# Padding of the weight buffers, start addresses of y and the mix, and the last three pieces by block

## The chip, the cores and the metric

The kernel runs on one core of one Trainium2 chip. The metric is the device time of one execution in microseconds. The kernel before took 2162.01 us, the median of three runs (2161.94 to 2162.14).

## The reference

A two-layer encoder over 256 positions of width 2048, in float32. Every layer is a pre-norm attention and a SwiGLU block of width 5632, both residual; layer 0 has two groups of heads (chunked and differential attention), layer 1 has attention over keys that an indexer selects. Nearly all the arithmetic is in the weight matrices:

```python
for layer in range(DEPTH):
    h = rmsnorm(x, attn_norm[layer])
    ...                                   # projections of h, attention, output projection
    x = x + mix
    h = rmsnorm(x, ffn_norm[layer])
    x = x + (jax.nn.silu(h @ w_gate[layer]) * (h @ w_up[layer])) @ w_down[layer]
return rmsnorm(x, final_norm)
```

## The kernel before

Every weight matrix is streamed once, in pieces of 128 rows by 1024 float32 (two tiles of 128 rows by 512 columns). `load_w` brings a piece into `wl` by a DMA on SyncE's queue; ScalarE rounds it to `wh` (line 145) and VectorE makes the remainder `wo` = `wl` - `wh` (line 146), so that a product of two float32 matrices becomes three products of rounded parts. `wh` and `wo` have three buffers each, which the pieces take in turn. TensorE does nothing but matmuls, and every matmul has a load of its stationary operand ahead of it (PEld in the profile).

Two routines hold nearly all of the matmuls.

- `gemm_t` (tiles `acc`): the weights are the stationary operand, the activations `xs` the moving one. A piece serves four output tiles; for each there is a quartet: two matmuls of 512 columns with the two halves of `wh`, then two of 256 columns with the two halves of `wo` (function `products`). So a piece is 16 matmuls. The gate and up projections, the queries and the keys run here.
- `gemm_n` (tiles `nat`): the activations are the stationary operand and the weights, `wh` or `wo`, the moving one, always 512 columns. For each half of a piece and each block of 128 positions there is a triple (`mm3`): high part by `wh`, high part by `wo`, low part by `wh`. A piece is 12 matmuls. The values (stationary `xs` or `c`), the two output projections (stationary `mix`) and the down projections (stationary `y`) run here.

The order of the work is written out by hand: attention, norms and transposes are cut into steps that `pump` issues between matmuls. The end of the kernel is `finish_block`, once for each block of 128 positions: it adds the last column group to the residual (line 312), squares it and sums it (lines 307 and 271), makes the norm's factor (lines 255 and 257), scales four column groups (lines 674 to 678) and stores each (line 679). In the last down projection `gemm_n` is called with `last=2`: all but the last two pieces go block by block within a piece, and the last two go first for block 0, then `done` is called for it, and then for block 1.

Start addresses, in bytes within a partition, follow from the order and the sizes of the tiles. Counted by 256 they are, before:

| tile | start by 256 | used as |
|---|---|---|
| `xs` | 128 | moving in `gemm_t`, stationary for the values of layer 0 |
| `wh`, `wo` (4,224 bytes each, so every next buffer lies 128 further) | in two pieces of three `wh` 64 and `wo` 192, in the third `wh` 192 and `wo` 64 | stationary in `gemm_t`, moving in `gemm_n` |
| the same for pieces of the values (64 bytes on, `OFF`) | `wh` 128 and `wo` 0, or `wh` 0 and `wo` 128 | moving |
| `y` in both layers | 64 | stationary |
| `mix` of layer 0, of layer 1 | 64, 192 | stationary |

All steps inside these tiles (512, 1024 and 2048 bytes) are multiples of 256. A spacer tile ahead of `mix` (`SP0`, `SP1`) and of `y` (`SPY`) sets where these start.

Of the kernel before, what the change touches and what calls it, by code (L numbers as in the profile page):

```python
# [14 lines left out]
F32R = mybir.dt.float32r  # L15
# [5 lines left out]
P = 128  # L21
# [4 lines left out]
FT = DFF // P  # L26
# [13 lines left out]
def encoder_kernel(  # L40
# [27 lines left out]
    wpool = ctx.enter_context(tc.tile_pool(name="wpool", bufs=1))  # L68
# [13 lines left out]
    def bank(shape, name):  # L82
        return psum.tile(shape, F32, name=name, tag="ps")


    OFF = 16
    SP0, SP1, SPY = 16, 16, 96
    UKO, UVO = 0, OFF
    OUT0 = [4, 5, 6, 7, 0, 1, 2, 3]
    QUADS = (2, 3, 0, 1)  # L90
# [11 lines left out]
    def moving(pieces):  # L102
        return ((src, OFF) for src in pieces)

# [25 lines left out]
    def load_w(cuts=1, between=None):  # L130
        src = next(stream, None)
        if src is None:
            return
        src, off = src if isinstance(src, tuple) else (src, 0)
        if before:
            before.popleft()()
        width = src.shape[-1]
        wl = wpool.tile([P, width], F32, name="wl", tag="wl", bufs=5)
        wh, wo = (wpool.tile([P, width + 2 * OFF], F32R, name=n, tag=n, bufs=3)[:, off:off + width] for n in ("wh", "wo"))
        for i in range(cuts):  # L140
            if between is not None:
                between(i)
            c = slice(i * width // cuts, (i + 1) * width // cuts)
            nc.sync.dma_start(out=wl[:, c], in_=src[:, c])
            latest["act"] = nc.scalar.activation(wh[:, c], wl[:, c], AF.Copy)  # L145
            nc.vector.tensor_tensor(out=wo[:, c], in0=wl[:, c], in1=wh[:, c].bitcast(F32), op=ALU.subtract)  # L146
        ahead.append((wh, wo))

    def next_w():
        while len(ahead) < 3:  # L150
            n = len(ahead)
            load_w()
            if len(ahead) == n:
                break
        return ahead.popleft()
# [4 lines left out]
    def pump(n=1):  # L160
        for _ in range(n):
            while steps:
                try:
                    next(steps[0])
                    break
                except StopIteration:
                    steps.popleft()
# [15 lines left out]
    def mm3(out, a, b, start, stop):  # L183
        (ah, al), (bh, bl) = a, b
        mm(out, ah, bh, start, False)
        mm(out, ah, bl, False, False)
        mm(out, al, bh, False, stop)
# [26 lines left out]
    def gemm_n(lhs, nk, order=None, last=0, done=None):  # L214

        banks = [bank([P, 512], f"nat{i}") for i in range(2)]
        order = list(range(nk // 2)) if order is None else order

        def block_products(b, i, w):
            wh, wo = w  # L220
            for j in range(2):
                h, l = lhs(2 * order[i] + j)
                t = slice(b * P, (b + 1) * P)
                c = slice(j * 512, (j + 1) * 512)
                mm3(banks[b], (h[:, t], l[:, t]), (wh[:, c], wo[:, c]),
                    i == 0 and j == 0, i == len(order) - 1 and j == 1)

        for i in range(len(order) - last):
            w = next_w()
            for b in range(2):  # L230
                block_products(b, i, w)
                pump()
        if last:
            ws = [next_w() for _ in range(last)]
            for b in range(2):
                for i, w in enumerate(ws):
                    block_products(b, len(order) - last + i, w)
                done(b, banks[b])
        return banks

    def pairs(act):
        return lambda kt: (act[:, kt, 0, :], act[:, kt, 1, :])
# [59 lines left out]
    def new_sums():  # L302
        return {"sums": small.tile([P, 2, 4], F32, name="sums", tag="sums", bufs=2)}
# [5 lines left out]
    def add_block(bk, b, g, st):  # L309

        c = xn[:, b, 512 * g:512 * g + 512]
        nc.vector.tensor_tensor(out=c, in0=bk, in1=c, op=ALU.add)
        add_squares(st, b, g)
# [15 lines left out]
    def add_residual(banks, g, gi, st):  # L329
        for b in range(2):  # L330
            add_block(banks[b], b, g, st)
        steps.append(transpose_steps(g, gi))
# [30 lines left out]
    def load_x(t, n):  # L363
        if t:
            nc.sync.dma_start(out=xt[:, t:t + n, :], in_=xT[:, t:t + n, :])
        for i in range(t, t + n):
            normalize(i, xt[:, i, :], 0)

    load_w(2, between=lambda i: load_x(i, 1))
    before.extend(partial(load_x, t, 2) for t in range(2, KT, 2))  # L370
    load_w(2)
    load_w(2)

# [243 lines left out]
    def ffn(st):  # L617

        with tc.tile_pool(name="ffn", bufs=1) as fp:
            fp.tile([P, SPY], F32, name="spacer")  # L620
            y = fp.tile([P, FT, 2, S], F32R, name="y")
            for g in range(FT // 4):
                gb = gemm_t(xs, KT)
                if g == 0:
                    drain()
                ga = fp.tile([P, 4, S], F32, name="ga", tag="ga", bufs=1)
                for n in range(4):
                    a = ga[:, n, :]
                    combined(a, gb[n])
                    nc.vector.tensor_tensor(out=a, in0=a, in1=st["rr"], op=ALU.mult)  # L630
                    th = fp.tile([P, S], F32, name="th", tag="th", bufs=3)
                    nc.scalar.activation(th, a, AF.Tanh, scale=0.5)  # L632
                    nc.vector.scalar_tensor_tensor(out=a, in0=th, scalar=1.0, in1=a, op0=ALU.add, op1=ALU.mult)  # L633
                    nc.gpsimd.tensor_tensor(out=a, in0=a, in1=st["rs"], op=ALU.mult)  # L634
                ub = gemm_t(xs, KT)
                for n in range(4):
                    t = 4 * g + n
                    a = ga[:, n, :]
                    u = fp.tile([P, S], F32, name="up", tag="up", bufs=2)
                    combined(u, ub[n])  # L640
                    nc.vector.tensor_tensor(out=a, in0=a, in1=u, op=ALU.mult)
                    split((y[:, t, 0, :], y[:, t, 1, :]), a)
            yield y, fp

    def ffn_layer(st, gi, last):
        out = new_sums()
        body = ffn(st)
        y, fp = next(body)
        if last:
            gf = fp.tile([P, D], F32, name="gf", tag="ga", bufs=1)  # L650
            nc.sync.dma_start(out=gf, in_=bass.AP(tensor=gfin.tensor, offset=gfin.offset, ap=[[0, P], [1, D]]))
        for g in range(4):
            fin = last and g == 3
            banks = gemm_n(pairs(y), FT, last=2 if fin else 0, done=partial(finish_block, out, gf) if fin else None)
            if not last:
                add_residual(banks, g, gi, out)
            elif not fin:
                for b in range(2):
                    add_block(banks[b], b, g, out)
                    c = slice(512 * g, 512 * g + 512)  # L660
                    nc.gpsimd.tensor_tensor(out=xn[:, b, c], in0=xn[:, b, c], in1=gf[:, c], op=ALU.mult)
        for _ in body:
            pass
        return out
# [15 lines left out]

    steps.append(norm_steps(st, "n1", 0.5))
    st = ffn_layer(st, 2, False)


# [9 lines left out]
    banks = [bank([P, 2, S], f"x{n}") for n in range(3)]  # L694
# [135 lines left out]

    steps.append(norm_steps(st, "n3", 0.5))
    ffn_layer(st, 4, True)


# [61 lines left out]
```

## Time and profile before

| | |
|---|---|
| median of three runs | 2162.01 us |
| the profiled execution, its span | 2161.7 us, 2159.9 us |
| TensorE busy | 2148.4 us, 99% of the span |
| granted TensorE clock | 0.999 of full speed |
| VectorE, ScalarE, GpSimd busy | 60%, 49%, 8% |
| DMA, mean busy share by slices | 50 to 60% in nearly all slices |

The span runs from the first instruction to the last. A matmul's row in the trace starts when its columns enter and ends when they have left, so that rows of matmuls one after the other overlap: the step from one start to the next is shorter than a row. PE is TensorE's matmuls, PEld its loads of stationary operands, DVE VectorE, ACT ScalarE, POOL GpSimd, SP SyncE, which here only issues DMAs.

### The profile page before, as it was taken

To read this page: it belongs to the slowest core of one execution; us is meant where nothing else is said; L and a number is where in the kernel's file an instruction comes from. 1 tells how busy PE (TensorE), PEld (TensorE's weight loads), DVE (VectorE), ACT (ScalarE), POOL (GpSimd) and SP (SyncE) were. 2 spreads that over 40 slices of the span, in tenths; PEclk is the share of its full clock that TensorE was granted. 3 is DMA by queue.
4 is the path that set the end of the run, shared out by engine and by line. 5 is a ranking of instruction groups with operands and counts; after the bars stand their busy time and mean duration, and the time that the engine had idled before them with its cause. 6 is when DMAs were issued, how large, how long until landed. Compare 5 with 4: busy or idle time off the path is not lost.

```text
span 2159.9 us, 29908 instructions
## 1 busy us (share of the span) xinstructions
PE 2148.4 (99%) x11380; PEld 1836.1 (85%) x11380; DVE 1299.2 (60%) x1882; ACT 1065.6 (49%) x1603; POOL 178.6 (8%) x194
## 2 busy tenths in 40 slices
PE   9999999999999999999999999999999999999998
PEld 8888888888888888888888888888888888888886
DVE  6665555666666666544446977556666666654443
ACT  6554554545454454444435566445454454543443
POOL 0111000000000000000001241000000000000000
PEclk9999999999999999999999999999999999999999
DMA  9565556555555665555656554555555555566564
GB/s 319 174 178 167 175 167 184 184 186 186 189 188 189 187 188 191 186 185 187 193 168 214 166 156 151 182 186 186 189 189 188 187 189 190 186 207 193 187 193 138
DMA packets 114975, 401.95 MB, mean 186 GB/s; under 512 B 12618, under 2 KB 16526, under 8 KB 114702
## 3 DMA queue, kind: packets, MB, share of 16 engines
q1 hardware_dynamic: 114686, 399.90, 58.7%
q8 instruction: 89, 1.46, 0.3%
q14 instruction: 56, 0.46, 0.1%
q10 hardware_dynamic: 144, 0.13, 0.0%
HBM read 397.84 MB, written 2.14 MB: 185 GB/s over the span
## 4 chain that ended last, share of the span: by engine, by line
PE 98%; DMA 1%; DVE 0%; ACT 0%; issue 0%; SPq 0%; ACTq 0%; POOLq 0%; POOL 0%
PE acc L181 59%; PE nat L181 35%; PE x L181 1%; PE uk L181 1%; DMA xt<-in_xT 1%; PE xT L323 0%; PE is L181 0%; PE c3o L181 0%; PE a0o L181 0%; PE a1o L181 0%; PE c2o L181 0%; PE c0o L181 0%; PE c1o L181 0%; DVE wo L146 0%; PE b31o L181 0%
## 5 line engine op out<-in xcount | busy, mean ns | idle before, releaser
L146 DVE TENSOR_TENSOR wo<-wl,wh 128x1024 fp32r<-128x1024 f32 (+2 forms) x747 | 925.9, 1240 | 805.2 <-ACT wh L145 797.3
L145 ACT ACTIVATE wh<-wl 128x1024 fp32r<-128x1024 f32 (+2 forms) x747 | 786.9, 1054 | 910.1 <-PE acc L181 491.9
L181 PE MATMUL acc<-xs,wh 128*128 128x512 f32 x3648 | 1147.7, 396 | 0.5 <-ACT wh L145 0.5
L181 PEld LDWEIGHTS acc<-xs,wo 128*128 128x128 f32 x3648 | 685.6, 188 | 160.2 <-DVE wo L146 1.6
L181 PE MATMUL acc<-xs,wo 128*128 128x256 f32 x3648 | 731.1, 281 | 0.6 <-DVE wo L146 0.5
L181 PEld LDWEIGHTS acc<-xs,wh 128*128 128x128 f32 x3648 | 560.3, 188 | 3.2 <-ACT wh L145 0.8
L181 PE MATMUL nat<-wh,y 128*128 128x512 f32 x1408 | 441.6, 394 | 0.0
L181 PEld LDWEIGHTS nat<-wh,y 128*128 128x128 f32 x1408 | 264.2, 188 | 61.4
L181 PE MATMUL nat<-wo,y 128*128 128x512 f32 x704 | 276.4, 393 | 0.0
L181 PE MATMUL nat<-wh,mix 128*128 128x512 f32 x512 | 166.7, 397 | 0.0
L181 PEld LDWEIGHTS nat<-wo,y 128*128 128x128 f32 x704 | 132.3, 188 | 29.8
L337 ACT ACTIVATE u<-acc 128x256 f32<-128x256 f32 x228 | 86.3, 379 | 61.4 <-PE acc L181 32.3
L181 PEld LDWEIGHTS nat<-wh,mix 128*128 128x128 f32 x512 | 96.1, 188 | 21.1
L181 PE MATMUL nat<-wo,mix 128*128 128x512 f32 x256 | 100.4, 392 | 0.0
L181 PE MATMUL nat<-wh,xs 128*128 128x512 f32 x256 | 83.2, 393 | 0.0
L634 POOL TENSOR_TENSOR ga<-ga,n1rs 128x256 f32<-128x256 f32 x44 | 37.7, 867 | 440.3 <-DVE ga L633 417.2
L634 POOL TENSOR_TENSOR ga<-ga,n3rs 128x256 f32<-128x256 f32 x44 | 36.6, 843 | 441.4 <-DVE ga L633 418.3
L181 PEld LDWEIGHTS nat<-wh,xs 128*128 128x128 f32 x256 | 48.1, 188 | 10.0
L181 PEld LDWEIGHTS nat<-wo,mix 128*128 128x128 f32 x256 | 48.2, 188 | 9.7
L181 PE MATMUL nat<-wo,xs 128*128 128x512 f32 x128 | 50.0, 391 | 0.0
L298 ACT ACTIVATE xs<-xT,gc 128x256 fp32r<-128x256 f32 x48 | 22.4, 467 | 31.0 <-DVE xs L299 31.0
L632 ACT ACTIVATE th<-ga 128x256 f32<-128x256 f32 x88 | 33.8, 410 | 5.8 <-DVE ga L630 5.7
(804 smaller groups left out, 1056.3 us busy)
## 6 DMA issues: line engine op xcount, KB each, us to landing
wl<-in_w_gate SPq DMA_DIRECT2D x176, 512.0 KB, 3.8
wl<-in_w_up SPq DMA_DIRECT2D x176, 512.0 KB, 3.6
wl<-in_w_down SPq DMA_DIRECT2D x176, 512.0 KB, 3.6
wl<-in_w_ein SPq DMA_DIRECT2D x93, 512.0 KB, 3.6
wl<-in_w_eout SPq DMA_DIRECT2D x32, 512.0 KB, 3.6
wl<-in_w_oq SPq DMA_DIRECT2D x32, 512.0 KB, 3.6
wl<-in_w_oout SPq DMA_DIRECT2D x32, 512.0 KB, 3.5
wl<-in_w_oi SPq DMA_DIRECT2D x8, 512.0 KB, 4.2
```

The costliest lines, as they stand in the source:

```text
L145: latest["act"] = nc.scalar.activation(wh[:, c], wl[:, c], AF.Copy)
L146: nc.vector.tensor_tensor(out=wo[:, c], in0=wl[:, c], in1=wh[:, c].bitcast(F32), op=ALU.subtract)
L181: nc.tensor.matmul(out, a, b, start=start, stop=stop, skip_group_check=True)
L298: nc.scalar.activation(xs[:, t, 0, :], src, AF.Copy, scale=g)
L337: nc.scalar.activation(u[:m], b[:m, 0, :], AF.Copy)
L632: nc.scalar.activation(th, a, AF.Tanh, scale=0.5)
L634: nc.gpsimd.tensor_tensor(out=a, in0=a, in1=st["rs"], op=ALU.mult)
```

## The change

Each buffer of `wh` and `wo` gets 256 bytes of padding and not 128, so that all six start at 64 by 256. The pieces of the values still lie 64 bytes on in theirs, so at 128, as `xs`. The spacers are set anew: `y` stays at 64 by 256 and `mix` is at 64 in both layers; the latent `c` of layer 1, behind its `mix`, moves from 0 to 128. In the last down projection the last three pieces, not two, go block by block.

```diff
-    OFF = 16
-    SP0, SP1, SPY = 16, 16, 96
+    OFF, PAD = 16, 64
+    SP0, SP1, SPY = 464, 112, 32
...
-        wh, wo = (wpool.tile([P, width + 2 * OFF], F32R, name=n, tag=n, bufs=3)[:, off:off + width] for n in ("wh", "wo"))
+        wh, wo = (wpool.tile([P, width + PAD], F32R, name=n, tag=n, bufs=3)[:, off:off + width] for n in ("wh", "wo"))
...
-            banks = gemm_n(pairs(y), FT, last=2 if fin else 0, done=partial(finish_block, out, gf) if fin else None)
+            banks = gemm_n(pairs(y), FT, last=3 if fin else 0, done=partial(finish_block, out, gf) if fin else None)
```

## Rows read from the trace of the kernel before

**Rows 1.** The page, its first part: busy us (share of the span) xinstructions.

```profile
PE 2148.4 (99%) x11380; PEld 1836.1 (85%) x11380; DVE 1299.2 (60%) x1882; ACT 1065.6 (49%) x1603; POOL 178.6 (8%) x194
```

**Rows 2.** TensorE by line, tile and shape: count, busy us, mean ns.

```profile
L181 PE MATMUL acc<-xs,wh 128*128 128x512 f32 x3648 | 1147.7, 396 | 0.5 <-ACT wh L145 0.5
...
L181 PE MATMUL nat<-wh,y 128*128 128x512 f32 x1408 | 441.6, 394 | 0.0
L181 PE MATMUL nat<-wo,y 128*128 128x512 f32 x704 | 276.4, 393 | 0.0
```

**Rows 3.** The chain that ended last: start us, us, piece of work.

```profile
410.50 479.55 PE acc L181 x2736
...
1349.27 19.36 PE nat L181 x84
...
1906.77 241.39 PE nat L181 x1044
```

**Rows 4.** TensorE's matmuls in order, two pieces of layer 0's FFN: start us, us.

```profile
497.28 0.63 PE L181 MATMUL acc<-xs,wh 128*128 128x512 f32 x2
...
498.68 0.62 PE L181 MATMUL acc<-xs,wh 128*128 128x512 f32 x2
...
500.07 0.62 PE L181 MATMUL acc<-xs,wh 128*128 128x512 f32 x2
...
501.47 0.63 PE L181 MATMUL acc<-xs,wh 128*128 128x512 f32 x2
...
502.18 0.63 PE L181 MATMUL acc<-xs,wh 128*128 128x512 f32 x2
...
502.88 0.63 PE L181 MATMUL acc<-xs,wh 128*128 128x512 f32 x2
```

**Rows 5.** All engines in order, near the end: a matmul and a load.

```profile
2143.34 0.40 PE L181 MATMUL nat<-wo,y 128*128 128x512 f32 x1
2143.34 0.42 PEld L181 LDWEIGHTS nat<-wh,y 128*128 128x128 f32 x2
```

**Rows 6.** TensorE by line inside the first of these pieces, 497.6 to 499.7 us.

```profile
L181 PE MATMUL acc<-xs,wh 128*128 128x512 f32 x8 | 2.5, 392 | 0.0
L181 PE MATMUL acc<-xs,wo 128*128 128x256 f32 x6 | 1.2, 282 | 0.0
```

**Rows 7.** The same inside the second, 500.4 to 502.5 us.

```profile
L181 PE MATMUL acc<-xs,wh 128*128 128x512 f32 x8 | 2.5, 395 | 0.0
L181 PE MATMUL acc<-xs,wo 128*128 128x256 f32 x6 | 1.2, 281 | 0.0
```

**Rows 8.** The same in a piece of the last down projection, 1934.8 to 1936.8 us.

```profile
L181 PE MATMUL nat<-wh,y 128*128 128x512 f32 x6 | 1.9, 394 | 0.0
L181 PE MATMUL nat<-wo,y 128*128 128x512 f32 x4 | 1.6, 391 | 0.0
```

**Rows 9.** The same in another piece there, 1940.3 to 1942.3 us.

```profile
L181 PE MATMUL nat<-wh,y 128*128 128x512 f32 x6 | 1.9, 392 | 0.0
L181 PE MATMUL nat<-wo,y 128*128 128x512 f32 x4 | 1.6, 389 | 0.0
```

**Rows 10.** All engines in order, the last 17 us.

```profile
2143.70 1.23 DVE L146 TENSOR_TENSOR wo<-wl,wh 128x1024 fp32r<-128x1024 f32 x1 [1.52 <-ACT wh L145]
...
2148.18 0.69 DVE L312 TENSOR_TENSOR xn<-nat,xn 128x512 f32<-128x512 f32 x1 [3.26 <-PE nat L181]
...
2150.53 0.40 PE L181 MATMUL nat<-wh,y 128*128 128x512 f32 x1
...
2151.08 0.75 DVE L674 SCALAR_TENSOR_TENSOR xn<-xn,n40r,gf 128x512 f32<-128x512 f32 x1
...
2151.74 0.69 DVE L312 TENSOR_TENSOR xn<-nat,xn 128x512 f32<-128x512 f32 x1
```

**Rows 11.** What TensorE's matmuls waited for: us, times, longest.

```profile
PE acc L181 <- DVE wo L146: 0.5, 1, 0.5
PE acc L181 <- ACT wh L145: 0.5, 1, 0.5
```

## The prediction

> **What bounds the kernel now.** I read the page first. TensorE is busy for 2148.4 of 2159.9 us [rows 1], and its matmuls waited for another engine for two times 0.5 us [rows 11] outside the warm-up at the start. So no DMA, conversion or norm sets the time; only the length of the matmuls does, and the few microseconds at both ends. VectorE and ScalarE have 40% and more to spare, so what the change does to the addresses that they read and write is hidden behind TensorE as long as a piece takes them less than TensorE.
>
> Then I read the chain that ended last for the step from one matmul to the next, which is what the time is made of. In layer 0's FFN 2,736 matmuls of `acc` follow each other in 479.55 us: 175.28 ns each, 701.1 ns a quartet [rows 3]. In the last down projection 1,044 of `nat` take 241.39 us: 231.2 ns each, 693.7 ns a triple. With the mix of layer 1 it is 19.36 us for 84, 230.5 ns each [rows 3]. A row of such a matmul is recorded as 393 or 394 ns [rows 2], so a row is a step plus some 163 ns; a difference of rows is a difference of steps.
>
> Then I asked whether all pieces cost the same, since the change only moves addresses. They do not. In two pieces that follow each other in the same projection, the first (`wh` at 192, `wo` at 64) goes from 497.28 to 500.07 us, 2.79 us; the second (`wh` at 64, `wo` at 192) from 500.07 to 502.88, 2.81 us [rows 4]. The quartets within them run from 1.39 us for two (498.68 to 500.07, 695 ns each) to 0.71 us for one (501.47 to 502.18) [rows 4]. Rows of `wh` are 392 ns in the first kind and 395 in the second, those of `wo` 282 and 281 [rows 6, 7]. Instructions, shapes and order are the same in both; what differs is where the buffers start. In the down projection the two kinds read 394 and 391 ns (`wh` at 64, `wo` at 192) against 392 and 389 (`wh` at 192, `wo` at 64) [rows 8, 9].
>
> What the reader is to take along: a load of weights starts with the matmul ahead of the one that it is for (2143.34 for both) [rows 5], so each matmul streams its moving operand while the next stationary one is read. I call the start of the moving operand less that of the stationary one being loaded, by 256, the lead. Before, leads in `gemm_t` are 64 where a part at 64 is loaded and 192 where one at 192 is; in `gemm_n` they are 0 and 128. The change makes them 64 throughout in `gemm_t` and 0 throughout in `gemm_n`.
>
> **The change part by part.**
>
> *`gemm_t`, 1,824 quartets (3,648 matmuls with `wh`, two a quartet [rows 2]).* A quartet loads two parts of `wh` and two of `wo`. After the change its `wh` lies as in the second kind of piece, its `wo` as in the first. No piece before has both, so the cost is bounded from two sides. If each load keeps its cost, the new quartet is half of the one and half of the other: (2.79 + 2.81) / 2 / 4 = 0.700 us, 1.1 ns under the mean of 701.1, times 1,824 is -2.0 us. Below: all quartets as the quickest seen, 695 ns, 6.1 x 1,824 = -11.1 us. Above: all as the slowest, 710 ns, +16.2 us. I take -2.0. One matmul of the four is new in the strict sense: the second of `wh`, which runs after a load at lead 64 and loads a `wo` at lead 64.
>
> *`gemm_n`, 3,264 matmuls (2,112 with `y` [rows 2], 768 with `mix`, 384 with `xs`: pieces times 12).* All go to lead 0. At lead 0 today are `wh` at 64 (394 ns) and `wo` at 64 (389); at lead 128 `wo` at 192 (391) and `wh` at 192 (392) [rows 8, 9]. Two `wh` to one `wo`, lead 0 throughout would be (2 x 394 + 389) / 3 = 392.3 and lead 128 throughout (2 x 392 + 391) / 3 = 391.7: less than 1 ns apart, and the stage's mean is (2 x 394 + 393) / 3 = 393.7. So by this I take 0. Above: pieces with two of three matmuls at lead 0 read (2 x 394 + 391) / 3 = 393.0, those with one 391.0; drawn out to three of three, 395.0, that is +1.3 ns on the stage's mean or +4.2 us. Below: every triple as in the faster kind, 391.0 or -2.7 ns, would be -8.8 us; the mix of layer 1 at 230.5 ns against 231.2 gives only -2.3. I keep +4.2 and -8.8 as ends.
>
> *Everything else that moves* (`c`, the heads' tiles, spacers): no instruction and no byte of DMA more. Matmuls of this kind (`uk`, `c`, scores) are under 300 of 11,380; at 2 ns each that is 0.6 us, which I leave out. The conversions of a piece are 1.23 us on VectorE [rows 10] in some 2.8 us of TensorE; were they half as long again they would still be hidden.
>
> *The last three pieces by block.* TensorE does the same 36 matmuls in another order. Block 0 is complete 6 matmuls earlier, 6 x 0.231 = 1.39 us. Now the last matmul ends at 2150.53 + 0.40 = 2150.93, but the addition for block 1 starts only at 2151.74, because VectorE is at block 0's last scaling from 2151.08 for 0.75 us [rows 10]. With block 0 earlier by 1.39 us that scaling ends near 2150.44, and the addition starts when TensorE is done: 0.8 us gained, which all that follows in block 1 (square, sum, power, scalings, stores) takes over unchanged. What can be late instead is the last piece: it is used 6 matmuls sooner, at about 2148.16 - 12 x 0.231 = 2145.39 for `wh` and a matmul later for `wo`, and its `wo` is ready at 2143.70 + 1.23 = 2144.93 [rows 10]. There is 0.5 us of room, so no wait. -0.8 us; 0 if the room is used up.
>
> **The sum.** -2.0 + 0 - 0.8 = -2.8 us on the profiled execution's 2161.7 (0.3 us under the median of 2162.01): **2158.9 us**. What can be told from no change is 0.2%, 4.3 us, so the forecast is no change, with a small gain in it.
>
> **The rivals.**
>
> *The leads, once equal, settle in the quickest pattern* (faster). Within the first piece the quartets go from 0.70 to 695 ns as it proceeds [rows 4]: a pattern of starts that needs some matmuls to settle, and that the next piece, with its buffers the other way round, breaks up. With one pattern for all pieces nothing breaks it. At 695 ns: 2161.7 - 11.1 - 0.8 = 2149.8; with the lower end of `gemm_n` 2141. Against it: what settled is `wo` at 64 with `wh` at 192, and after the change `wh` is at 64.
>
> *The new matmul is a slow one* (slower). In the second kind of piece it is the `wh` rows that are long [rows 7], and one quartet takes 710 ns. If lead 64 after lead 64 puts every quartet there, `gemm_t` pays 16.2 us: 2161.7 + 16.2 - 0.8 = 2177.1. It decides for slower from (4.3 + 0.8) / 1,824 = 2.8 ns, a quartet of 704 ns.
>
> *The addresses do nothing.* The 0.02 us between the pieces could come from something else that has a period of three pieces, such as when the conversions read and write. Then only the tail counts: 2160.9. For it: the difference is under 1%. Against it: 392 and 395 ns inside the pieces, with the same conversions going on beside both [rows 6, 7].
> The Trainium skill, "SBUF — State Buffer", section "Who interferes with whom", would have it so: TensorE has two independent read ports, one for the moving operand and one for weights, and never waits on anyone. By that rule the time would be 2160.9. The trace doesn't agree: quartets of 695 and 710 ns differ in nothing but start addresses [rows 4].
>
> **How the numbers follow.** Forecast (2154 to 2165) 0.48; quickest pattern 0.27; slow matmul 0.15; nothing 0.10. Of the forecast's own range about a third lies below 2157.7, where it counts as faster, and a tenth is slower. Faster: 0.27 + 0.15 = 0.42. Slower: 0.15 + 0.04 = 0.19. Same: 0.39. The range takes in the quickest pattern with a little of `gemm_n`'s gain (2161.7 - 11.1 - 0.8 - 4 = 2146) and, above, a part of the slow rival; what lies beyond 2145 and 2167 I put at 2 in 10.
>
> **What would show it.** The steps from the chain: `acc` 175.0 ns (700 a quartet) and `nat` 231.2. All pieces of one projection alike, with no third piece shorter; 2.80 us each in `gemm_t`. At the end, block 1's addition within 0.05 us of the last matmul, and no wait of TensorE for the last piece. The prediction is wrong if a uniform lead has a cost that is not the mean of the two that it was mixed from: then `acc` shows it first, 1 ns a matmul there being 7.3 us.

## The result and the profile after

The kernel after takes 2130.66 us, the median of four runs (2130.61 to 2131.42), against 2161.98 (2161.85 to 2162.14): 0.9856 of the time, with an interval of 0.9839 to 0.9873. The forecast was 2158.9, its range 2145 to 2167. The kernel is faster by 31.3 us, about ten times what was forecast, and lies 14 us below the range.

The page of the kernel after, its first part, as in [rows 1]:

```profile
span 2128.9 us, 29908 instructions
...
PE 2117.0 (99%) x11380; PEld 1824.4 (86%) x11380; DVE 1301.5 (61%) x1882; ACT 1066.8 (50%) x1603; POOL 178.5 (8%) x194
```

As many matmuls as before are busy for 31.4 us less, somewhat more than the span lost (31.0 us); the granted clock is 0.999 as before. So the matmuls follow each other faster, and no wait went away.

TensorE by line, tile and shape (count, busy us, mean ns, idle before), as in [rows 2]:

```profile
L181 PE MATMUL acc<-xs,wh 128*128 128x512 f32 x3648 | 1139.2, 393 | 0.9 <-ACT wh L145 0.9
...
L181 PE MATMUL nat<-wh,y 128*128 128x512 f32 x1408 | 435.6, 390 | 0.0
L181 PE MATMUL nat<-wo,y 128*128 128x512 f32 x704 | 273.9, 389 | 0.0
```

Rows are 3 or 4 ns shorter, and waits are still below a microsecond. The chain that ended last has the steps, as in [rows 3] (start us, us, piece of work):

```profile
406.34 471.97 PE acc L181 x2736
...
944.54 57.17 PE nat L181 x252
...
1332.27 19.09 PE nat L181 x84
...
1409.33 471.97 PE acc L181 x2736
1881.30 235.32 PE nat L181 x1038
```

A step of `acc` is 471.97 / 2736 = 172.50 ns (175.28 before): 690.0 ns a quartet on the average, where the quickest that I had seen was 695. A step of `nat` with `y` is 235.32 / 1038 = 226.7 ns (231.2 before), with the mix of layer 1 227.3 (230.5). TensorE's matmuls in order, two starts a row (start us, us), in the stretch of [rows 4]:

```profile
500.03 0.62 PE L181 MATMUL acc<-xs,wh 128*128 128x512 f32 x2
...
500.72 0.62 PE L181 MATMUL acc<-xs,wh 128*128 128x512 f32 x2
...
501.41 0.62 PE L181 MATMUL acc<-xs,wh 128*128 128x512 f32 x2
...
502.10 0.62 PE L181 MATMUL acc<-xs,wh 128*128 128x512 f32 x2
...
502.79 0.62 PE L181 MATMUL acc<-xs,wh 128*128 128x512 f32 x2
```

Every quartet takes 0.69 us and every piece 2.76; no third piece is different any more. At the end, first VectorE and then TensorE in order, as in [rows 10]:

```profile
2119.53 0.74 DVE L674 SCALAR_TENSOR_TENSOR xn<-xn,n40r,gf 128x512 f32<-128x512 f32 x1
...
2120.72 0.69 DVE L312 TENSOR_TENSOR xn<-nat,xn 128x512 f32<-128x512 f32 x1 [0.44 <-PE nat L181]
```

```profile
2120.29 0.39 PE L181 MATMUL nat<-wh,y 128*128 128x512 f32 x1
```

Block 1's addition starts 0.04 us after the end of the last matmul (2120.68), where it was 0.81 us: block 0's scaling is over by then.

Where the 31.0 us of span came from, by the starts of stretches in the two chains: 4.2 us ahead of layer 0's FFN (410.50 to 406.34), 21.3 from there to the last down projection, in which the two stretches of `acc` give 7.6 each, and 5.5 behind that: 1,044 matmuls at 4.5 ns are 4.7, the tail 0.8. The `acc` of the attention has the step of the FFN too: one of its stretches, from the chain of before and then of after:

```profile
97.75 30.85 PE acc L181 x176
```

```profile
97.28 30.36 PE acc L181 x176
```

That is 175.3 and 172.5 ns.

### The profile page after: what moved, and what is told of

Its sections match the earlier page's. It is cut to its first block, busy times and chain, and to the rows that moved or that the text cites. A ratio compares the mean times of both kernels' runs of the same rounds, so it can differ in the third digit from the quotient of the medians.

```text
span 2128.9 us, 29908 instructions
## 1 busy us (share of the span) xinstructions
PE 2117.0 (99%) x11380; PEld 1824.4 (86%) x11380; DVE 1301.5 (61%) x1882; ACT 1066.8 (50%) x1603; POOL 178.5 (8%) x194
## 4 chain that ended last, share of the span: by engine, by line
PE 97%; DVE 1%; DMA 1%; POOL 0%; issue 0%; ACT 0%; SPq 0%; POOLq 0%; ACTq 0%
PE acc L181 58%; PE nat L181 35%; PE x L181 1%; DMA xt<-in_xT 1%; PE uk L181 1%; PE xT L323 0%; DVE wo L146 0%; PE is L181 0%; DVE sc L780 0%; POOL tm L789 0%; DVE m L779 0%; PE c3o L181 0%; PE a1o L181 0%; PE a0o L181 0%; PE c2o L181 0%
## 5 line engine op out<-in xcount | busy, mean ns | idle before, releaser
L181 PE MATMUL acc<-xs,wo 128*128 128x256 f32 x3648 | 722.8, 279 | 0.9 <-DVE wo L146 0.8
L181 PEld LDWEIGHTS acc<-xs,wh 128*128 128x128 f32 x3648 | 554.3, 188 | 3.8 <-ACT wh L145 1.6
L181 PE MATMUL nat<-wh,y 128*128 128x512 f32 x1408 | 435.6, 390 | 0.0
```

The costliest lines, as they stand in the source:

```text
L181: nc.tensor.matmul(out, a, b, start=start, stop=stop, skip_group_check=True)
```

## The experiments

Two questions were open. Which part did it? And what about the addresses: that there is one lead and nothing changes from piece to piece, or the lead's own value; and does each load have a cost of its own that adds up, as the prediction had it?

### The two parts alone

`e4_tail` is the kernel before with the last three pieces by block:

```diff
-            banks = gemm_n(pairs(y), FT, last=2 if fin else 0, ...)
+            banks = gemm_n(pairs(y), FT, last=3 if fin else 0, ...)
```

> The kernel before with the last three pieces by block and nothing else. All theories: 0.8 us less than before, 2161.2 us, block 1's addition at the end starting when the last matmul is done. If the last piece comes too late: TensorE waits for it near the end, and less is gained.

Measured: 2161.19 us (ten runs, 2160.97 to 2161.71) against 2162.12 (thirteen), 0.9996 with an interval of 0.9986 to 1.0005. By the times alone that can't be told from nothing; the trace has it. VectorE and then TensorE at the end of `e4_tail`:

```profile
2150.00 0.75 DVE L674 SCALAR_TENSOR_TENSOR xn<-xn,n40r,gf 128x512 f32<-128x512 f32 x1
...
2151.29 0.69 DVE L312 TENSOR_TENSOR xn<-nat,xn 128x512 f32<-128x512 f32 x1 [0.54 <-PE nat L181]
```

```profile
2150.85 0.40 PE L181 MATMUL nat<-wh,y 128*128 128x512 f32 x1
```

0.04 us from the last matmul's end to the addition, as in the kernel after: the term of the tail stands, at 0.8 to 0.9 us.

`e7_padding_alone` is the kernel after with two pieces by block as before; the other spacer puts the mix of layer 1 at 192, so lead 128, and `c` back at 0:

```diff
-    SP0, SP1, SPY = 464, 112, 32
+    SP0, SP1, SPY = 464, 80, 32
...
-            banks = gemm_n(pairs(y), FT, last=3 if fin else 0, ...)
+            banks = gemm_n(pairs(y), FT, last=2 if fin else 0, ...)
```

> The kernel after without two of its parts: two last pieces by block and not three, and the mix of layer 1 left at 192 (c at 0), as before; the padding of the buffers stays, so gemm_t is at lead 64 and gemm_n at 0 but for layer 1's output projection (128). From the stages measured so far: 2130.7 + 0.9 for the tail + 384 x (232.5 - 227.3 ns) = 2.0 us for that projection: 2133.6 us. If the parts do not add up, over 2135 or under 2132.

Measured: 2133.51 us (four runs, 2133.15 to 2133.74), 0.9868 with an interval of 0.9851 to 0.9884. So the addresses of the weights' buffers bring 28.6 us of the 31.3. Its chain, the mix of layer 1 and the FFN behind it:

```profile
1332.46 19.59 PE nat L181 x84
...
1410.98 471.97 PE acc L181 x2736
```

The mix of layer 1 takes 233.2 ns a matmul at lead 128, against 227.3 at lead 0; with that, layer 1's FFN starts 1.65 us later than in the kernel after (1410.98 against 1409.33). Of the 2.5 us between the two profiled spans (2131.4 and 2128.9) the other 0.9 is the tail. Here only `mix` moved and the weights stayed at 64, and the time comes within 0.7 ns of the mix at lead 128 in `e1_leads_a` below (232.5), where the weights move; so in `gemm_n` it is the difference of the two starts that counts. The values of layer 0, with both starts at 128, have the step of lead 0 too: 6.82 us for 30 matmuls in the kernel after, 227.3 ns.

### One lead for a whole stage

The next kernels are the kernel after with the buffers' starts set stage by stage: `t` gate and up, `n` down, `m` the output projections, each for layers 0 and 1. A pair is the offset of `wh` and of `wo` in floats; the lead is 64 - 4 x offset in `gemm_t` and 4 x offset in `gemm_n`, by 256. All the rest of the kernel after stays. `e1_leads_a`:

```diff
+    PLACES = {('t', 0): [(16, 16)], ('t', 1): [(48, 48)], ('n', 0): [(16, 16)], ('n', 1): [(32, 32)], ('m', 0): [(48, 48)], ('m', 1): [(32, 32)]}
+    def at(kind, layer, pieces):
+        places = PLACES[kind, layer]
+        return ((p, places[i % len(places)]) for i, p in enumerate(pieces))
...
-            yield from (w_gate[layer, g, k] for k in range(KT // 2))
+            yield from at("t", layer, (w_gate[layer, g, k] for k in range(KT // 2)))
...
+        offs = off if isinstance(off, tuple) else (off, off)
-        wh, wo = (wpool.tile(...)[:, off:off + width] for n in ("wh", "wo"))
+        wh, wo = (wpool.tile(...)[:, o:o + width] for n, o in zip(("wh", "wo"), offs))
```

> The kernel after, with the pieces put further on in their buffers, so that the leads are uniform within each stage but other than 64 (gemm_t) and 0 (gemm_n): FFN of layer 0 gemm_t at lead 0, of layer 1 at 128; down projection of layer 0 at lead 64, of layer 1 at 128; output projection of layer 0 at 192, of layer 1 at 128. After has 172.5 ns a matmul in gemm_t and 226.7 in gemm_n, before 175.3 and 231.2. Theory 'one relation': any lead will do as long as it is the same for all loads, so gemm_t is near 172.5 in both layers and gemm_n near 227 in all four stages. Theory 'right lead': only the leads of the kernel after are quick, so gemm_t is at 175 or more at one of the two leads at least, gemm_n at 231 or more.

Measured: 2153.38 us. Its chain (start us, us, piece of work):

```profile
409.24 476.53 PE acc L188 x2736
...
1342.03 19.53 PE nat L188 x84
...
1420.46 476.53 PE acc L188 x2736
1896.99 242.21 PE nat L188 x1038
```

One lead is not enough: at lead 0 and at 128 `acc` takes 174.17 ns, at 64 it is 172.50. The last down projection at lead 128 takes 233.3 ns, more than the mixture before (231.2). The value matters. But the other theory's figure for `gemm_t`, 175 or more, was missed as well: both leads lie between the kernel after and the kernel before. In `gemm_t` no run moves `xs`, so what is listed below by lead could there as well go by the start of `wh` and `wo` itself; that is not shown.

`e6_fine` goes to other values:

```diff
+    PLACES = {('t', 0): [(8, 8)], ('t', 1): [(56, 56)], ('n', 0): [(56, 56)], ('n', 1): [(24, 24)], ('m', 0): [(1, 1)], ('m', 1): [(40, 40)]}
```

> The kernel after with leads not tried yet, uniform in each stage. FFN gemm_t at 32 (layer 0) and 96 (layer 1); down projection at 224 and 96; output projection at 4 and 160. Theory 'right lead': nothing here is under the 172.5 of lead 64 and the 226.7 of lead 0; 32 and 96 lie between or above their neighbours, 172.5 to 175 in gemm_t, 229 to 235 in gemm_n; lead 4, which shares no line with lead 0 at its ends, 228 to 234. Theory 'one relation', already hit by the runs before, would have all near 172.5 and 227. If one is quicker than the kernel after, a better version can be made of it.

Measured: 2164.15 us, 2.0 us more than the kernel before beside it, though every one of these stages has one lead. In its chain, the mix of layer 0 at lead 4, then the two FFNs' `acc` at 32 and 96, and the last down projection at 96:

```profile
330.65 19.93 PE nat L188 x84
...
410.23 474.25 PE acc L188 x2736
...
1424.39 483.36 PE acc L188 x2736
1907.75 242.22 PE nat L188 x1038
```

That is 237.3, 173.34, 176.67 and 233.35 ns. Lead 4 and, in `gemm_t`, lead 96 came out slower than the bounds that were set for them (234 and 175). All single leads that ran, in ns a matmul (from the chains' stretches; the mix at 64 is from `e2_leads_b`, and the leads 16 in `e3_leads_c`, 48 in `e9_odd_piece` and 240 and 256 in `e5_turns` are among them):

| lead by 256 | 0 | 4 | 16 | 32 | 48 | 64 | 96 | 128 | 160 | 192 | 224 | 240 |
|---|---|---|---|---|---|---|---|---|---|---|---|---|
| `gemm_t`, FFN | 174.2 | | | 173.3 | 175.0 | 172.5 | 176.7 | 174.2 | | 173.3 | | |
| `gemm_n`, `y` | 226.7 | | | 233.3 | | 229.0 | 233.4 | 233.3 | | 233.3 | 233.4 | |
| `gemm_n`, mix | 227.3 | 237.3 | 231.7 | 233.3 | | 229.1 | | 232.5 to 233.2 | 234.2 | 233.3 | | 236.7 |

The mix at lead 256 took the same 19.09 us as at 0. The kernel after has the least of each row.

### Two leads in a piece

`e2_leads_b`, `e3_leads_c` and `e8_two_leads` set `wh` and `wo` apart in some stages:

```diff
+    PLACES = {('t', 0): [(32, 32)], ('t', 1): [(0, 32)], ('n', 0): [(48, 48)], ('n', 1): [(0, 32)], ('m', 0): [(16, 16)], ('m', 1): [(32, 0)]}
```

> As the run before it, with other leads. FFN of layer 0 gemm_t at lead 192; of layer 1 with wh at lead 64 and wo at 192 in every piece (the second kind of piece of before, without the third piece that had them the other way round). Down projection of layer 0 at lead 192; of layer 1 with wh at lead 0 and wo at 128 in every piece. Output projection of layer 0 at lead 64, of layer 1 with wh at 128 and wo at 0. 'One relation': lead 192 gives 172.5 and 227 as after; the mixed leads stay slow although all pieces are alike, 175.6 (2.81 us a piece) in gemm_t and 231 in gemm_n. Rival 'turns between pieces': the buffers' turning round from piece to piece is what cost, so mixed leads that are alike in all pieces are quick too, 173 and 227 to 228. 'Right lead': 192 is slow.

```diff
+    PLACES = {('t', 0): [(32, 0)], ('t', 1): [(0, 0), (32, 32)], ('n', 0): [(0, 0), (32, 32)], ('n', 1): [(32, 0)], ('m', 0): [(8, 8)], ('m', 1): [(4, 4)]}
```

> As the two before it. FFN of layer 0 gemm_t with wh at lead 192 and wo at 64 in every piece (the first kind of before, settled); of layer 1 with both parts at lead 64 in one piece and at 192 in the next, by turns. Down projection of layer 0 with both parts at lead 0 in one piece and 128 in the next, by turns; of layer 1 with wh at 128 and wo at 0 in every piece. Output projection of layer 0 at lead 32, of layer 1 at lead 16, which no whole 64 bytes make up. 'One relation': the mixed stages stay slow (layer 0 gemm_t 173.4, the settled 693 ns a quartet; down projection of layer 1 229), the stages with turns are quick inside a piece and pay a little at each border, 173 and 227.5. 'Turns between pieces': the other way round, stages with turns at 175 and 231. Leads 32 and 16: as quick as 0 if only equality counts, slower if a line of 64 bytes counts.

```diff
+    PLACES = {('t', 0): [(0, 16)], ('t', 1): [(16, 0)], ('n', 0): [(0, 16)], ('n', 1): [(16, 0)], ('m', 0): [(0, 48)], ('m', 1): [(48, 0)]}
```

> The kernel after with wh and wo at different leads of the better kind, the same in all pieces, to see whether a pair beats one lead for both. gemm_t: wh 64 and wo 0 (layer 0), wh 0 and wo 64 (layer 1). Down projection: wh 0 and wo 64, wh 64 and wo 0. Output projection: wh 0 and wo 192, wh 192 and wo 0. If the cost is one price for each lead: 173.3 in both layers of gemm_t, 227.4 and 228.2, 229 and 231. If the pattern as a whole decides, as the runs before show (wh 128 with wo 0 was quicker than lead 128 and than wh 0 with wo 128): totals that are whole steps of 6.7 ns a triple or quartet, some perhaps under the kernel after: 226.7 or 224.5 in gemm_n, 171.7 in gemm_t.

Measured: 2148.01, 2143.72 and 2151.16 us. The chain of `e2_leads_b`, layer 1's FFN with `wh` at lead 64 and `wo` at 192, then the down projection with 0 and 128:

```profile
1419.73 474.24 PE acc L188 x2736
1893.96 239.90 PE nat L188 x1038
```

and that of `e3_leads_c`, in layer 0 one of the groups of the down projection with single leads of 0 and 128 by turns, in layer 1 an FFN with single leads of 64 and 192 by turns, then a down projection with 128 and 0:

```profile
950.38 58.01 PE nat L188 x252
...
1418.86 473.12 PE acc L188 x2736
1891.98 237.60 PE nat L188 x1038
```

In `e8_two_leads`, layer 0's `acc` with 64 and 0 and its down projection with 0 and 64, then layer 1's with 0 and 64 and with 64 and 0:

```profile
406.71 477.66 PE acc L188 x2736
...
952.04 58.46 PE nat L188 x252
...
1422.86 474.26 PE acc L188 x2736
1897.12 239.91 PE nat L188 x1038
```

If each load had a cost of its own, a pair would lie at the weighted mean of its single leads:

| leads of `wh`, `wo` | by the mean, ns | measured, ns |
|---|---|---|
| `gemm_t` 64, 192 (and 192, 64) | 172.9 | 173.3 (173.3) |
| `gemm_t` 64, 0 | 173.3 | 174.6 |
| `gemm_t` 0, 64 | 173.3 | 173.3 |
| `gemm_n` 0, 128 | 228.9 | 231.1 |
| `gemm_n` 128, 0 | 231.1 | 228.9 |
| `gemm_n` 0, 64 | 227.5 | 232.0 |
| `gemm_n` 64, 0 | 228.2 | 231.1 |
| `gemm_n`, mix 128, 0 | 230.8 to 231.2 | 229.2 |
| `gemm_n`, mix 0, 192 | 229.3 | 229.3 |
| `gemm_n`, mix 192, 0 | 231.3 | 234.5 |

The mean holds for two of these pairs and fails for the others, while stretches of the same leads repeat to 0.04 us. In `gemm_n` with 0 and 128 it has the two the wrong way round: there `wh`, two of three matmuls, is better off at 128 when `wo` is at 0. Two prices, one for `wh` and one for `wo`, do no better. By them the two single leads of a pair would together take what the two mixed ones take. For 0 and 128 in `gemm_n` they do (226.7 + 233.3 and 231.1 + 228.9, 460.0 both), but 0 and 64 take 455.7 alone and 463.1 mixed, and in `gemm_t` 64 and 192 take 345.8 and 346.7, 64 and 0 take 346.7 and 347.9. Nor are all mixtures quick once pieces stop turning round, as the rival 'turns between pieces' had it: 231.1 ns for 0 and 128 is hardly less than before. What adds up is whole pieces with one lead each: 64 and 192 by turns take 473.12 us, 172.92 ns, just the mean of 172.50 and 173.34. The down projection of layer 0 with 0 and 128 by turns takes 58.01 us for 252, 230.2 ns, where the mean is 230.1.

### The turns of the pieces

`e5_turns` lets the places run on from call to call. Layer 0 has just the leads of before, two pieces one way and the third the other, in buffers that all start at 64. In layer 1 one piece of eight is the other way round:

```diff
+    PLACES = {('t', 0): [(0, 32), (0, 32), (32, 0)], ('t', 1): [(32, 0), (0, 32), (0, 32), (0, 32), (0, 32), (0, 32), (0, 32), (0, 32)], ('n', 0): [(0, 32), (0, 32), (32, 0)], ('n', 1): [(0, 32), (32, 0)], ('m', 0): [(64, 64)], ('m', 1): [(60, 60)]}
+    turn = {key: cycle(places) for key, places in PLACES.items()}
+    def at(kind, layer, pieces):
+        return ((p, next(turn[kind, layer])) for p in pieces)
```

> The kernel after with its uniform buffers, the pieces placed in them so that the leads of before come back by offsets alone. FFN of layer 0 gemm_t and down projection of layer 0: two pieces with wh at lead 64 and wo at 192 (0 and 128 in the down projection) and one the other way round, and so on, as before. Theory 'the leads make the time, whatever sets them': 175.3 ns in gemm_t and 231.2 in gemm_n, as before. Rival 'the buffers' own places (their stride, the conversions that write them)': near 172.5 and 227, or near the 173.3 and 229 to 231 of the mixed but regular stages. FFN of layer 1 gemm_t: one piece the other way round, then seven with wh at 64 and wo at 192. If the odd piece only costs itself: 173.4. If it throws the next seven into another pattern that holds, as the quartets of 0.70 and 0.71 us of before: 175 to 176. Down projection of layer 1: the two kinds by turns, between 229 and 232. Output projection of layer 0 at lead 256: as at 0, 227.3; of layer 1 at 240: if only multiples of 64 are quick, 230 or more.

Measured: 2158.46 us. Its chain:

```profile
406.70 479.56 PE acc L190 x2736
...
1424.49 480.38 PE acc L190 x2736
1904.87 239.48 PE nat L190 x1038
```

The 479.56 us are those of before [rows 3] to 0.01 us, and so is the time of the down projection of layer 0, here one group of it in `e5_turns` and then in the kernel before:

```profile
1015.60 58.28 PE nat L190 x252
```

```profile
1019.51 58.28 PE nat L181 x252
```

The leads alone make the time, not where the buffers otherwise lie. And the second line of `acc` is news: one odd piece in eight brings 474.24 us to 480.38, though pieces of either kind take 474.25 when they are alone. TensorE in order there, first starts of the odd piece, of the next and of the one behind it:

```profile
1522.55 0.63 PE L190 MATMUL acc<-xs,wh 128*128 128x512 f32 x2
...
1525.34 0.62 PE L190 MATMUL acc<-xs,wh 128*128 128x512 f32 x2
...
1528.15 0.63 PE L190 MATMUL acc<-xs,wh 128*128 128x512 f32 x2
```

The odd piece takes 2.79 us and the next 2.81, as in [rows 4], and so do all seven behind it. The same piece with nothing odd near it, in `e2_leads_b`:

```profile
1522.17 0.62 PE L188 MATMUL acc<-xs,wh 128*128 128x512 f32 x2
...
1524.95 0.62 PE L188 MATMUL acc<-xs,wh 128*128 128x512 f32 x2
```

2.78 us by these two rows, 2.77 on the average. In `e5_turns` itself the pieces ahead of the first odd one of this stretch, which follow four small matmuls of another kind (`n3p`), still take 2.77 us for four quartets:

```profile
1427.10 0.62 PE L190 MATMUL acc<-xs,wh 128*128 128x512 f32 x2
...
1429.87 0.62 PE L190 MATMUL acc<-xs,wh 128*128 128x512 f32 x2
```

So pieces with two leads have more than one rhythm that lasts, and an odd piece throws them into the slow one.

`e9_odd_piece` does that to pieces with one lead, one of eight in layer 1's `acc` and one of eleven in layer 0's down projection:

```diff
+    PLACES = {('t', 0): [(4, 4)], ('t', 1): [(32, 32), (0, 0), (0, 0), (0, 0), (0, 0), (0, 0), (0, 0), (0, 0)], ('n', 0): [(32, 32), (0, 0), (0, 0), (0, 0), (0, 0), (0, 0), (0, 0), (0, 0), (0, 0), (0, 0), (0, 0)], ('n', 1): [(8, 8)], ('m', 0): [(0, 0)], ('m', 1): [(0, 0)]}
```

> The kernel after with one odd piece now and then at its own leads: in layer 1 one piece of gemm_t of eight at lead 192 and seven at 64; in layer 0 one piece of eleven of the down projection at 128 and ten at 0. If the quick pattern of a single lead comes back by itself after an odd piece: 172.6 and 227.3. If the odd piece throws it out, as it did for the mixed leads: 174 or more, 229 or more. gemm_t of layer 0 at lead 48: if a line of 64 bytes counts, over 174. Down projection of layer 1 at lead 32: 233, as in the output projection.

Measured: 2145.26 us. Its chain:

```profile
951.48 57.34 PE nat L190 x252
...
1416.63 472.25 PE acc L190 x2736
```

Against the kernel after (57.17 and 471.97 us) that is 0.28 us for some 21 odd pieces of `acc`, 0.013 each, and what lead 192 costs such a piece by itself is 16 x 0.84 = 13 ns. With one lead an odd piece, at lead 192 here, costs its own time and leaves nothing behind.

## Why the prediction was wrong

- **What bounds the kernel:** right. TensorE's matmuls one after the other set the time before and after, and conversions, norms and DMAs stayed hidden.
- **The leads set the step:** right, and shown for the start addresses: `e5_turns` has the steps of before with uniform buffers and the leads of before. That it is the difference of two starts is shown for `gemm_n` alone (`e7_padding_alone`).
- **`gemm_t`, "if each load keeps its cost", -2.0 us: the step that failed.** A load has no cost of its own that it would keep with another neighbour: by such costs 64 and 192 mixed would take 345.8 ns in the sum of the two pairs, and they take 346.7. The prediction had named this as what would show it wrong, a uniform lead that doesn't cost the mean of the two that it was mixed from. Nor did the sum price the new quartet: the middle of the two kinds still has half of its loads at lead 192, and the rows that it could have gone by, 395 ns for `wh` at 64 and 282 for `wo` at 64 [rows 6, 7], are the longer of each, so that added up they gave more than either kind. The step fell by 2.78 ns a matmul, 11.1 a quartet; the two FFN stretches alone gave 15.2 us. By the runs, 175.28 to 173.34 ns comes from the end of the turns (`e2_leads_b`, `e3_leads_c`: two leads, but the same in every piece), and 173.34 to 172.50 from lead 64 in all four matmuls. The lower end failed for the same reason: 695 ns was the quickest quartet of a mixture, and no bound for a quartet that no piece before had.
- **`gemm_n`, 0:** the second place where that step failed. The rows [rows 8, 9] told which kind of piece is quicker (393.0 against 391.0 ns; alone 231.1 against 228.9), but I shared them out to leads and read lead 0 as the slower one, while alone it is the quickest, 226.7, and lead 128 one of the slow, 233.3. Of 231.2 to 226.7 ns, 0.8 comes from the end of the turns ((2 x 231.1 + 228.9) / 3 = 230.4) and 3.7 from lead 0. By its steps that is 9.4 us with `y` (1,056 in each layer, at 4.4 and 4.5), 1.2 and 1.6 with the mix of layer 1 and of layer 0 (384 each, at 3.2 and 4.1), 1.0 with the values (384 x 2.6), 13.2 in all.
- **The tail, -0.8:** right in place and size.
- **What is left:** 15.2 + 13.2 + 0.8 = 29.2 of the 31.0 us. The four long stretches of `acc` in layer 0's attention, 696 matmuls at 2.7 ns, give the other 1.9. That is the sum to 0.1 us; the short groups and the start, 0.3 us later, were not taken apart.
- **The rivals:** "settle in the quickest pattern" was right in part: the end of the turns is 1.9 of 2.8 ns in `gemm_t`, but 0.8 of 4.5 in `gemm_n`, and equal leads of some other values are slower than before (176.7 at 96, 233.3 at 128). Its time (2149.8, or 2141 with `gemm_n`) was too high, since it took its prices from the mixture. That what breaks the rhythm is the turn of the third buffer is shown by `e5_turns` against `e2_leads_b`. "The new matmul is a slow one" did not happen at lead 64; at lead 96 in all four matmuls a quartet takes 706.7 ns, over the 704 that it named. "The addresses do nothing" is out. The Trainium skill, "SBUF — State Buffer", section "Who interferes with whom", has TensorE's two operands read through independent ports and TensorE waiting on no one. Taken to mean that a load and the matmul beside it can't hold each other up, it does not fit the traces, with 690.0 to 706.7 ns for the same quartet by start addresses alone; the ports themselves no run shows.
- **Open:** what in the chip ties a load and the matmul that runs beside it to their addresses by 256. No run looks at that; only the steps are measured.

## What to carry to other kernels

When TensorE's matmuls follow each other without a wait and each has its own load, look in the chain at the step of a stretch, and in the timeline at whether identical pieces take the same time; if they don't, print where the moving and the stationary tile start, by 256, and give all buffers of one use the same start. Then try a few starts, each in a stage of its own so that one run prices several: equal starts alone can be slower than a mixture (233.3 against 231.2 ns), and the best lead depends on the sequence of matmuls (0 for triples of 512 columns, 64 for quartets of 512 and 256). A price read from a mixture is no bound for a new combination: the range has to say so, however small the differences in the mixture are.

## What the runs showed of the hardware

- A float32-rounded matmul of 512 columns with a load ahead of each took 226.7 to 237.3 ns by the lead alone; a lead of 4 bytes was the slowest (237.3), with 231.7 at 16, and lead 256 was as quick as 0 (19.09 us for 84 both).
- Many totals that repeat lie on steps of some 6.7 ns, which is 16 cycles at 2.4 GHz (the granted clock was 0.999): triples of 680.1, 686.9, 693.4 and 700.0 ns, quartets of 693.3, 700.0 and 706.7. Not all do: quartets of 690.0 and 696.7 lie half a step off, and 698.3 (leads 64 and 0) on neither. Why there are such steps is open.
- The rhythm has a memory: with two leads in a piece, pieces of the same instructions and addresses took 2.77 us, or 2.81 for all seven pieces up to the next odd one, by what one piece ahead of them had been.
